# Selection and gates of a product-key expert layer by quarters of the tokens, and the sum over experts in three steps

## The chip, the cores and the metric

The kernel runs on one NeuronCore of a Trainium2 chip. Its time is the device time of one execution in microseconds (us), the median of several. Five engines execute instruction streams of their own and wait for each other through semaphores: TensorE (PE; its weight loads are listed apart, as PEld), VectorE (DVE), ScalarE (ACT), GpSimd (POOL) and SyncE (SP), which here issues the DMA transfers. Each engine works off its stream in order.

## The reference

Two layers. Each adds a token mixer (window attention, stick-breaking attention and gated linear attention beside each other) to the activations of 16 meta and 1024 real tokens, 1024 wide, and then a PEER layer with 4096 experts. Only the PEER layer matters here:

```python
q = (xt @ wq).reshape(t, 8, 2, 128)
s = jnp.einsum('thpd,hpnd->thpn', q, sub_keys)             # 8 heads, 2 halves, 64 keys
s_top, i_top = lax.top_k(s, 16)
cand_s = s_top[:, :, 0, :, None] + s_top[:, :, 1, None, :] # 16 x 16 candidates of a head
best_s, best_j = lax.top_k(cand_s, 16)
g = jax.nn.softmax(best_s, axis=-1)                        # 8 x 16 gates of a token
h_all = xt @ u.T                                           # 4096 hidden values of a token
a = gelu(h_sel) * g                                        # those of the 128 selected experts
w = zeros((t, 4096)).at[token, idx].add(a)
out = w @ v                                                # the sum over experts
```

All products are in float32. The kernel computes all 4096 hidden values of every token, multiplies them with a gate that is zero for an expert that is not selected, and sums over all experts.

## The kernel before

A float32 product is computed as three products of operands split in a high and a low part. `wpiece` loads a 128 x 512 piece of weights; ACT rounds it to the high part (L272) and POOL or DVE subtracts to get the low part (L279; `split_on` says which engine). A piece with a key is kept: its low part goes to memory and is loaded again at the next use, and ACT rounds again (L306).

The 1040 tokens stand in four quarters (272, 256, 256, 256; in the last layer the first is 256, since the meta tokens are dropped). After the attention of a layer its PEER layer goes over a first pair of quarters, P, and then a second, Q. For each pair there are these stages:

- `apply` writes the norm of a quarter (DVE L373 and L377, ACT L376).
- `scores` multiplies it with the keys (PE L977) in four blocks of two heads each, c = 0 to 3, and ACT copies the result to SBUF (L982).
- `route` selects, for one block and both quarters: the sixteen largest of each list of 64 (DVE L994 to L998, five instructions to a list), the candidates (L1010 to L1017), their sixteen largest, the softmax (Exp on ACT, L1029) and the numbers of the experts (L1047 to L1082).
- `hidden`: 32 rounds of 128 experts. PE L1101 multiplies both quarters at once, 24 matmuls of 512 columns to a round; ACT takes the Gelu (L1107, L1110), and where a token's gate is there already, POOL multiplies it in (L1108).
- `slots` transposes the selected numbers and gates (PE L1120 to L1125, DVE L1122 to L1129).
- `gates` makes the gates of 16 tokens for all experts: DVE compares the numbers with a ramp (L1140, 128x2048; L1143, 128x512; L1145, 128x1024), PE forms the outer products in 32 matmuls of 32 columns (L1152), and DVE multiplies them into the hidden rows that are there (L1157), ACT copies them for those that are not (L1159). A pair of 512 tokens has 32 such blocks.
- `values` sums over the experts for four output tiles, d0 to d0 + 3, at a time, with 32 rounds: ACT and DVE split the 128x512 gated rows (L1185, L1186), PE L1191 multiplies with 12 matmuls, and at the end DVE adds the result to the activations (L259) and POOL sums squares for the next norm (L255).

For P, all of `route` and `slots` come ahead of round 17 of hidden (PR), and the 32 gate blocks are spread over rounds 17 to 28 (PEND is 29, and what is due by then is issued at the end of a round). The norms, scores and `route` of Q are laid between the rounds of the two values passes of P, one work item to EVERY / 4 = 6 rounds: norms at rounds 6 and 12, the scores at 18, 24, 30 and 36 of 64. `route` goes between them in portions (BUD). For Q, `slots` comes after round HQ = 6 of hidden and the gates are spread to round 31 (QE). A scheduler that works at build time orders the instructions of each engine from these programs by its own estimates of their times; on the chip the order is fixed. PSUM banks are handed out by rings, named in `set_rings`: h for hidden, g for gates and slots, s and d for scores, v for values.

Of the kernel before, what the change touches and what calls it, by code (L numbers as in the profile page):

```python
# [61 lines left out]
def tile_trunk(ctx, tc, h0, w_pk, wgate, w2, glab, w_out, wqT, keysT, u_pk, v_w, sinks,  # L62
# [52 lines left out]
    kb, bb = place["keep"][1], place["beta"][1]  # L115
    place["hq"] = [1, [kb[0]], 0]
# [54 lines left out]
    set_rings(d=(0, 1), o=(2,), a=(3, 4, 5, 6, 7), h=(0, 1, 6, 7), g=(2, 3), s=(2, 3, 4, 5), v=(4, 5, 6, 7, 2, 3))  # L171
# [762 lines left out]
    def peer_setup(qa, qb):  # L934

        P = Layer()
        P.sp = sp = Span(qa.c0, qb.c1)
# [18 lines left out]
    def scores(l, P, c, halves, ring):  # L956

        sp = P.sp
        if P.s[c] is None:
            P.s[c] = sb([128, P.ns, len(sp.tiles), 4, 64], F32, "s")[:, c % P.ns]  # L960
            if sp.meta:
                POOL.memset(P.s[c][:, 0], 0.0)
# [454 lines left out]
```

## Time and profile before

| | |
|---|---|
| median of 3 runs | 3347.84 us (3345.78 to 3351.06) |
| profiled execution | 3347.21 us, span 3345.5 us |
| PE busy | 3140.4 us, 94% |
| DVE busy | 2107.7 us, 63% |
| ACT busy | 1311.3 us, 39% |
| POOL busy | 938.1 us, 28% |
| granted TensorE clock, mean | 0.961 of 2.4 GHz |

Times in the trace are from the start of the span. Layer 0 has P's hidden stage at 765 to 1045, P's values at 1045 to 1306, Q's hidden at 1306 to 1523 and its values, with the first projection of layer 1, to 1785. Layer 1 has the same stages at 2426, 2684, 2930 and 3143 us, to the end. A row of a group of instructions gives its line, engine, operation, output and input by the program's names, shapes, count, busy time and mean ns, and then the idle time of the engine ahead of it with what ended that. A share of busy time is an average over stages with different limits, so the rows below are by stage.

### The profile page before, as it was taken

Reading aid. Unit: us, or ns where it says so; the run is one execution under the profiler, and the core shown is the slowest. Engines: PE = TensorE matmul, PEld = TensorE weight load, DVE = VectorE, ACT = ScalarE, POOL = GpSimd, SP = SyncE. Lnnn points to the kernel's source line nnn. Section 1 sums busy time; section 2 is a strip of 40 time slices with the busy share of each in tenths; the row PEclk is TensorE's granted clock in tenths of the full one; section 3 lists DMA queues with packets and bytes.
Section 4 is the critical chain, followed back from the end, with each engine's and each line's share of the span. In section 5 each row is a group of like instructions: output and inputs, shape, how many; then the busy total and the mean of one; then the engine's idle time right before and its main releaser. Section 6 shows DMA issues by size and latency. Waiting matters only on the chain.

```text
span 3345.5 us, 65752 instructions
## 1 busy us (share of the span) xinstructions
PE 3140.4 (94%) x23483; PEld 2642.3 (79%) x23483; DVE 2107.7 (63%) x6764; ACT 1311.3 (39%) x3021; POOL 938.1 (28%) x963
## 2 busy tenths in 40 slices
PE   7999999989799989999998999999898899999998
PEld 7686887679799988888875868876776778688788
DVE  4645436569997589653325464465697867975447
ACT  4544324433223434324344343245342244333345
POOL 4314021214344233010311131223143433311125
PEclk9899999989899999999997999999898999999999
DMA  8767774655335655446874677756754366554655
GB/s 290 228 208 245 238 261 135 199 188 187 124 117 158 183 178 190 155 152 200 311 251 151 216 263 238 253 160 201 233 177 139 115 181 219 182 187 145 194 177 160
DMA packets 397225, 651.36 MB, mean 195 GB/s; under 512 B 43536, under 2 KB 109152, under 8 KB 396896
## 3 DMA queue, kind: packets, MB, share of 16 engines
q1 hardware_dynamic: 396896, 647.16, 60.1%
q8 instruction: 184, 3.01, 0.4%
q14 instruction: 145, 1.19, 0.1%
HBM read 489.56 MB, written 157.42 MB: 193 GB/s over the span
## 4 chain that ended last, share of the span: by engine, by line
PE 61%; DVE 21%; DMA 6%; ACT 2%; issue 2%; POOL 1%; SPq 0%; DVEq 0%; POOLq 0%; ACTq 0%
PE b L1191 15%; PE b L1101 14%; PE b L333 11%; PE b L977 4%; PE b L1152 3%; PE b L703 2%; DVE arena_r L1186 2%; DMA arena<-h 2%; DVE arena L995 2%; DVE arena L996 2%; PE b L757 1%; DVE arena L998 1%; PE b L618 1%; DVE arena L1140 1%; DVE arena L1145 1%
## 5 line engine op out<-in xcount | busy, mean ns | idle before, releaser
L279 POOL TENSOR_TENSOR arena_r<-arena,arena_r 128x512 fp32r<-128x512 f32 (+1 forms) x453 | 557.6, 1238 | 915.0 <-ACT arena_r L272 843.8
L1101 PE MATMUL b<-arena_r 128*128 128x512 f32 (+2 forms) x3840 | 766.4, 359 | 22.9 <-ACT arena L1110 13.4
L1191 PE MATMUL b<-arena_r 128*128 128x512 f32 (+2 forms) x4224 | 752.5, 337 | 31.9 <-DVE arena_r L1186 22.1
L1191 PEld LDWEIGHTS b<-arena_r 128*128 128x128 f32 x4224 | 642.6, 190 | 128.9 <-DVE arena_r L1186 37.2
L1101 PEld LDWEIGHTS b<-arena_r 128*128 128x128 f32 x3840 | 630.7, 193 | 123.0 <-ACT arena L1110 14.0
L333 PE MATMUL b<-arena_r 128*128 128x256 f32 (+1 forms) x4992 | 700.9, 294 | 27.5 <-ACT arena_r L272 6.3
L333 PEld LDWEIGHTS b<-arena_r 128*128 128x128 f32 x4992 | 641.0, 195 | 67.1 <-issue 20.4
L272 ACT ACTIVATE arena_r<-arena 128x512 fp32r<-128x512 f32 x456 | 285.0, 629 | 447.3 <-PE b L1101 93.7
L1186 DVE TENSOR_TENSOR arena_r<-arena,arena_r 128x512 fp32r<-128x512 f32 (+2 forms) x352 | 258.1, 743 | 215.6 <-ACT arena_r L1185 214.8
L306 ACT ACTIVATE arena_r<-arena 128x512 fp32r<-128x512 f32 x284 | 178.5, 631 | 359.8 <-PE b L1191 118.0
L977 PE MATMUL b<-arena_r 128*128 128x256 f32 (+1 forms) x1632 | 219.1, 290 | 17.9 <-DMA arena_r<-m_0l 6.4
L977 PEld LDWEIGHTS b<-arena_r 128*128 128x128 f32 (+1 forms) x1632 | 204.2, 190 | 30.9 <-DMA arena_r<-m_0l 8.5
L1140 DVE TENSOR_TENSOR arena<-arena 128x2048 f16<-128x2048 f16 x129 | 172.4, 1338 | 59.7 <-PE b L1152 59.7
L1108 POOL TENSOR_TENSOR arena<-arena 128x272 f32<-128x272 f32 (+26 forms) x86 | 90.0, 1051 | 372.5 <-ACT arena L1159 177.5
L1185 ACT ACTIVATE arena_r<-arena 128x512 fp32r<-128x512 f32 (+2 forms) x352 | 171.8, 502 | 24.1 <-PE b L1191 24.1
L1152 PEld LDWEIGHTS <-arena 128*128 128x128 f16 x4128 | 144.9, 118 | 36.9 <-DVE arena L1145 20.8
L1152 PE MATMUL b<-arena 128*128 128x32 f16 x4128 | 154.0, 190 | 18.9 <-DVE arena L1145 18.8
L255 POOL TENSOR_TENSOR arena<-arena 128x256 f32<-128x256 f32 (+2 forms) x105 | 90.7, 864 | 260.5 <-ACT arena L254 256.0
L715 DVE TENSOR_TENSOR_SCAN arena<-arena,zf 128x384 f32<-128x384 f32 (+6 forms) x116 | 104.5, 904 | 82.0 <-ACT arena L710 81.0
L279 DVE TENSOR_TENSOR arena_r<-arena,arena_r 128x256 fp32r<-128x256 f32 (+1 forms) x187 | 98.0, 528 | 89.7 <-ACT arena_r L272 72.0
L421 ACT ACTIVATE arena<-b 128x256 f32<-128x256 f32 (+1 forms) x144 | 55.4, 385 | 212.3 <-PE b L333 211.8
L1157 DVE SCALAR_TENSOR_TENSOR arena<-b,arena 128x288 f32<-128x288 f32 (+21 forms) x129 | 63.7, 499 | 111.6 <-PE b L1152 111.6
(268 smaller groups left out, 3877.9 us busy)
## 6 DMA issues: line engine op xcount, KB each, us to landing
arena<-in_v_w_dram SPq DMA_DIRECT2D x288, 256.0 KB, 2.9
arena<-in_u_pk_dram SPq DMA_DIRECT2D x256, 256.0 KB, 3.0
arena_r<-a_0h SPq DMA_DIRECT2D x108, 256.0 KB, 3.6
arena_r<-a_0l SPq DMA_DIRECT2D x108, 256.0 KB, 3.9
arena_r<-a_1h SPq DMA_DIRECT2D x108, 256.0 KB, 3.0
arena_r<-a_1l SPq DMA_DIRECT2D x108, 256.0 KB, 3.5
arena<-m SPq DMA_DIRECT2D x92, 256.0 KB, 4.4
arena<-in_w_pk_dram SPq DMA_DIRECT2D x72, 256.0 KB, 4.3
```

The costliest lines, as they stand in the source:

```text
L272: ACT.activation(hi, src, AF.Copy)
L279: e.tensor_tensor(lo[:, a:b], src[:, a:b], hi[:, a:b].bitcast(F32), op=ALU.subtract)
L306: ACT.activation(hi, wload(src), AF.Copy)
L333: PE.matmul(ps, wt[:, ks], x.at(low, k, xo, sp.w), start=(k == 0 and i == 0), stop=(k == KT - 1 and i == 2))
L715: DVE.tensor_tensor_scan(keep[0:m, 0:wd][:, ::-1], keep[0:m, 0:wd][:, ::-1], zf[0:m, 0:1].to_broadcast([m, wd]), keep[0:m, wd:wd + 1], op0 ...
L977: PE.matmul(ps, yv(half, low, k, oo, m), wt[:, kk * 256:kk * 256 + 256], start=(k == 0 and i == 0 and e == 0), stop=(k == KT - 1 and i == ...
L1101: PE.matmul(ps, wt[:, ks], yv(h, low, k, 0, w // 2 if h is None else w), start=(k == 0 and i == 0), stop=(k == KT - 1 and i == 2))
L1140: DVE.tensor_tensor(Lh, iotaM.unsqueeze(1).to_broadcast([128, 4, 128, 4]), v4(P.mT, 128), op=ALU.is_equal)
L1152: PE.matmul(ps[:, i * 32:(i + 1) * 32], Lh[:, b, :, t], R[:, b, part, :, t], start=(part == 0), stop=(part == 1))
L1185: ACT.activation(ah, G[:, r, o:o + w], AF.Copy)
L1186: last = DVE.tensor_tensor(al, G[:, r, o:o + w], ah.bitcast(F32), op=ALU.subtract)
L1191: PE.matmul(ps, wt[:, d * 128:d * 128 + 128], pr[low], start=(opens and r == 0 and i == 0), stop=(closes and r == 31 and i == 2))
```

## The change

Selection goes by quarter and by two pairs of heads (`tops`, `combine`) instead of by pair of quarters and by score block. The gate blocks of a pair's first quarter stay in `hidden`, from round 15 to 30; those of its second quarter (`second`) go into the first pass of values, which then handles the first quarter only. The sum over experts has three steps: output tiles 0 to 3 for the first quarter, tiles 4 to 7 for both quarters, and tiles 0 to 3 for the second. The weights of tiles 0 to 3 are loaded and split afresh in each of these steps (`reuse=False`). Value matmuls of 512 columns go from 1920 to 1152, those of 256 from 1536 to 3072. The norms of both quarters of Q are at round 1 of the first values pass and its score blocks at rounds 8, 14, 20 and 26 of it; its selection is in the second and third pass and inside Q's hidden stage. The bank rings are new. The low parts of the weights are on POOL throughout the PEER layer, but for Q's second and third step, where POOL and DVE share a piece. The attention is not touched.

```diff
-BUD = 0.3
 LAG = 1
-EVERY = 24
-HQ = 6
-PR = 17
+PR = 15
 START = 0
 MM = ((3, 0, 2, 0, 0, 3, 0, 0), (3, 0, 2, 0, 0, 3, 0, 0))
-PEND = 29
-QE = 31
+PEND = 31
...
-    set_rings(d=(0, 1), o=(2,), a=(3, 4, 5, 6, 7), h=(0, 1, 6, 7), g=(2, 3), s=(2, 3, 4, 5), v=(4, 5, 6, 7, 2, 3))
+    set_rings(d=(0, 1), o=(2,), a=(3, 4, 5, 6, 7), h=(6, 7, 2, 3), g=(0, 1), s=(4, 5), v=(4, 5, 6, 7, 2, 3))
...
+    def tops(P, half, cc):
+
+        nt = len(P.parts[half][1].tiles)
+        V = sb([128, 3, 8, 16], F32, "V")
+        I = sb([128, 3, 8, 16], U32, "I")
+        P.V[half, cc] = V, I
+        for a in range(8):
+            for j in range(nt):
+                top16(sv(P, half, 2 * cc + a // 4)[:, j, a % 4, :], V[:, j, a], I[:, j, a])
+                yield 1.3
...
+    def combine(P, half, cc, startT, pidxT):
+
+        nt = len(P.parts[half][1].tiles)
+        ng = 4 * nt
+        z = "s" if half else ""
+        V, I = P.V.pop((half, cc))
...
+            w0 = P.parts[0][1].w
+            while cst and P.gated[0] < w0 and P.gated[0] * (end - lo) < w0 * (r + 1 - lo):
+                gates(P, 0, G, *cst)
...
+    def second(P, G, cst):
+
+        while P.gated[1] < P.parts[1][1].w:
+            gates(P, 1, G, *cst)
+            yield 3.0
+
+    def values(l, P, G, halves, d0, todo=iter(()), work=(), bud=0.0, hs=None, reuse=True):
...
+            if r in work:
+                work.pop(r)()
+            if len(done) > LAG:
+                left += bud
+                with tc.issue_after(done[-1 - LAG]):
+                    while left > 0:
+                        left -= next(todo, 99)
...
-        scores(l, P, P.ns - 1, (0,), "s")
+        scores(l, P, 3, (0,), "s")
...
+        def run(*gens):
+            for _ in itertools.chain(*gens):
+                pass
+
+        for c in range(3):
             scores(l, P, c, (1,), "s")
-            with tc.issue_after(A.done):
-                route(P, c, startT, pidxT)
-        hidden(l, P, G, 0, 4, "h")
-        for c in range(P.ns, 4):
-            scores(l, P, c, (0, 1), "s")
-            route(P, c, startT, pidxT)
-        hidden(l, P, G, 4, PR, "h")
-        slots(P)
+        with tc.issue_after(A.done):
+            run(tops(P, 0, 0), combine(P, 0, 0, *tabs), tops(P, 0, 1))
+            scores(l, P, 3, (1,), "s")
+            run(combine(P, 0, 1, *tabs))
+        hidden(l, P, G, 0, PR, "h")
+        slots(P, 0)
+        run(tops(P, 1, 0), tops(P, 1, 1))
         hidden(l, P, G, PR, 32, "h", cst, PEND)
+        run(combine(P, 1, 0, *tabs), combine(P, 1, 1, *tabs))
+        slots(P, 1)
         Q = peer_setup(qs[2], qs[3])
-        split_on(POOL)
-        todo = iter(())
-        work = [lambda: apply(2 * l + 1, qs[2], gf, Y[0], rb), lambda: apply(2 * l + 1, qs[3], gf, Y[1], rb2)]
-        work += [lambda c=c: scores(l, Q, c, (0, 1), "d") for c in range(4)]
-        step = 0
-        done = []
-        for d in (0, 4):
-            for last in values_steps(l, P, G, (0, 1), d):
-                done.append(last)
-                step += 4
-                if work and step >= EVERY:
-                    work.pop(0)()
-                    step = 0
-                    if len(work) < 4:
-                        todo = itertools.chain(todo, route_steps(Q, 3 - len(work), startT, pidxT))
-                if len(work) < 4:
-                    left = BUD * 4
-                    with tc.issue_after(done[-1 - LAG]):
-                        while left > 0:
-                            left -= next(todo, 9)
-        for _ in todo:
-            pass
-        split_on(POOL)
-        hidden(l, Q, G, 0, HQ, "h")
-        slots(Q)
-        split_on(*QSPL)
-        hidden(l, Q, G, HQ, 32, "h", cst, QE)
+        scored = []
+
+        def norms():
+            apply(2 * l + 1, qs[2], gf, Y[0], rb)
+            apply(2 * l + 1, qs[3], gf, Y[1], rb2)
+
+        work = {6 * c + 8: lambda c=c: scored.append(scores(l, Q, c, (0, 1), "g")) for c in range(4)}
+        work[1] = norms
+        todo = values(l, P, G, (0,), 0, second(P, G, cst), work, 2.2, reuse=False)
+        run(todo)
+        todo = itertools.chain(tops(Q, 0, 0), combine(Q, 0, 0, *tabs), tops(Q, 0, 1), combine(Q, 0, 1, *tabs))
+        todo = values(l, P, G, (0, 1), 4, todo, (), 1.8)
+        todo = values(l, P, G, (1,), 0, todo, (), 0.8, reuse=False)
+        run(todo)
+        hidden(l, Q, G, 0, PR, "h")
+        slots(Q, 0)
+        run(tops(Q, 1, 0), tops(Q, 1, 1))
+        hidden(l, Q, G, PR, 32, "h", cst, PEND)
+        run(combine(Q, 1, 0, *tabs), combine(Q, 1, 1, *tabs))
+        slots(Q, 1)
         more = l + 1 < DEPTH
         if more:
             rb = rstd(2 * l + 2, quarters[0])
             apply(2 * l + 2, quarters[0], g_attn[:, l + 1], XR[0], rb)
-        split_on(POOL, POOL, DVE, POOL)
+        todo = second(Q, G, cst)
+        run(itertools.islice(todo, 5))
+        todo = values(l, Q, G, (0,), 0, todo, (), 2.0, reuse=False)
+        run(todo)
         if more:
-            values(l, Q, G, (0, 1), 0)
             L = attn_layer(l + 1)
             pr = proj_span(l + 1, L, quarters[0], XR[0])
             A = next(pr)
             split_on((POOL, DVE))
             rb = rstd(2 * l + 2, quarters[1])
...
+            values(l, Q, G, (0, 1), 4)
             next(pr)
-            values(l, Q, G, (0, 1), 4)
+            values(l, Q, G, (1,), 0, reuse=False)
...
+        split_on((POOL, DVE))
+        values(l, Q, G, (0, 1), 4, work={2 + 8 * i: lambda i=i: final(qs[i]) for i in range(2)}, hs=hs)
...
+        values(l, Q, G, (1,), 0, work={4: lambda: final(qs[2])}, hs=hs, reuse=False)
```

The first place where the order moves is DVE in layer 1 while PE computes the first scores of P; L373 and L377 are the norm of P's second quarter, L355 and L360 the preparation of its factors. Before:

```order
L355 TENSOR_SCALAR arena<-b_66 128x2 x2
L360 TENSOR_SCALAR arena<-ident,arena 128x128 x3
L373 SCALAR_TENSOR_TENSOR arena<-arena,g_ffn 128x256
L360 TENSOR_SCALAR arena<-ident,arena 128x128
L377 TENSOR_TENSOR arena_r<-arena,arena_r 128x256
L373 SCALAR_TENSOR_TENSOR arena<-arena,g_ffn 128x256
L377 TENSOR_TENSOR arena_r<-arena,arena_r 128x256
L373 SCALAR_TENSOR_TENSOR arena<-arena,g_ffn 128x256 x2
```

In the change the same norm is L379 and L383, and L997 to L1001, L1041 to L1087 and L1064 are selection:

```order
L999 MATCH_REPLACE arena<-arena 128x64 x2
L1064 SCALAR_TENSOR_TENSOR arena<-arena 128x16x8
L1046 RECIPROCAL arena<-arena 128x8
L379 SCALAR_TENSOR_TENSOR arena<-arena,g_ffn 128x256
L1081 TENSOR_TENSOR arena<-arena 128x256x8
L1000 MAX arena<-arena 128x8 x8
L1065 TENSOR_SCALAR arena<-arena 128x16x8
L1047 TENSOR_TENSOR arena<-arena 128x2x64
L379 SCALAR_TENSOR_TENSOR arena<-arena,g_ffn 128x256 x2
L383 TENSOR_TENSOR arena_r<-arena,arena_r 128x256
```

The norm stood as a closed group between the selection before it and after it; it now has selection instructions among its own.

The second place is DVE in layer 1 where P's hidden ends and its values begin. L1140, L1145 and L1157 are the end of the last gate blocks, L1186 low parts, L373 and L377 the norm of Q's first quarter. Before:

```order
L1140 TENSOR_TENSOR arena<-arena 128x2048
L1145 TENSOR_TENSOR arena<-arena 128x1024
L1157 SCALAR_TENSOR_TENSOR arena<-b_68,arena 128x29x16
L1157 SCALAR_TENSOR_TENSOR arena<-b_67,arena 128x29x16
L1186 TENSOR_TENSOR arena_r<-arena,arena_r 128x512 x2
L373 SCALAR_TENSOR_TENSOR arena<-arena,g_ffn 128x256
L377 TENSOR_TENSOR arena_r<-arena,arena_r 128x256
L373 SCALAR_TENSOR_TENSOR arena<-arena,g_ffn 128x256
```

In the change L1172 is the product of a gate block, L1206 a low part (256 wide), L379 and L383 the norm, L1136 to L1143 the slots and L1155, L1158 and L1160 the gate blocks of the second quarter:

```order
L1172 SCALAR_TENSOR_TENSOR arena<-b_65,arena 128x31x16
L383 TENSOR_TENSOR arena_r<-arena,arena_r 128x256
L1206 TENSOR_TENSOR arena_r<-arena,arena_r 128x256 x4
L379 SCALAR_TENSOR_TENSOR arena<-arena,g_ffn 128x256 x2
L383 TENSOR_TENSOR arena_r<-arena,arena_r 128x256 x2
L1136 COPY arena<-b_66 128x128
L1137 COPY arena<-b_66 128x128
L1155 TENSOR_TENSOR arena<-arena 128x2048 x2
L1158 TENSOR_TENSOR arena<-arena 128x512 x2
L1143 SCALAR_TENSOR_TENSOR arena<-b_65,arena 128x32x4
```

No gate block was left here; now the slots and gate blocks of the second quarter stand among the norms and the low parts.

The third place is ACT at the start of P's hidden in layer 1. L1110 is a Gelu, L1029 an Exp of `route`, L272 the high part of a weight piece. Before, the second of four Exps:

```order
L272 ACTIVATE arena_r<-arena 128x512 x2
L1110 ACTIVATE arena<-b_65 128x512
L272 ACTIVATE arena_r<-arena 128x512 x2
L1110 ACTIVATE arena<-b_66 128x512
L272 ACTIVATE arena_r<-arena 128x512
L1029 ACT_TABLE_LOAD
L1029 ACTIVATE arena<-arena 128x128
L272 ACTIVATE arena_r<-arena 128x512
L1110 ACT_TABLE_LOAD
```

In the change L1124 is the Gelu, L1043 the Exp, L278 and L312 high parts of weights and L993 the copy of scores:

```order
L1043 ACTIVATE arena<-arena 128x128
L312 ACTIVATE arena_r<-arena 128x512 x4
L993 ACTIVATE arena<-b_70 128x512
L278 ACTIVATE arena_r<-arena 128x512 x4
L993 ACTIVATE arena<-b_69 128x512
L278 ACTIVATE arena_r<-arena 128x512 x3
L1124 ACT_TABLE_LOAD
L1124 ACTIVATE arena<-b_71 128x512
```

The first two of the four Exps now stand ahead of the first Gelu, where before one stood after the first, sixth, tenth and thirteenth Gelu.

## Rows read from the trace of the kernel before

**Rows 1.** Page, part 1: busy us, share of the span, instructions.

```profile
PE 3140.4 (94%) x23483; PEld 2642.3 (79%) x23483; DVE 2107.7 (63%) x6764; ACT 1311.3 (39%) x3021; POOL 938.1 (28%) x963
```

**Rows 2.** Busy time by stage: from:to, length, engines in turn, clock, DMA.

```profile
765.00:1045.30 280.30, 253.50 (x2730) 249.55 (x2729) 258.35 (x900) 85.43 (x202) 126.16 (x89) 0.95 0.41 133
1045.30:1306.50 261.20, 244.77 (x1928) 238.86 (x1927) 197.10 (x931) 106.00 (x249) 88.58 (x68) 0.98 0.59 181
...
2426.40:2683.70 257.30, 224.13 (x1806) 182.61 (x1804) 223.70 (x741) 80.17 (x161) 113.33 (x78) 0.91 0.43 139
2683.70:2930.20 246.50, 236.10 (x1167) 193.77 (x1168) 191.32 (x884) 97.44 (x183) 92.22 (x65) 0.98 0.64 200
2930.20:3143.40 213.20, 213.20 (x1794) 174.65 (x1793) 127.13 (x287) 74.72 (x166) 26.80 (x28) 1.00 0.52 164
...
2377.50:2409.50 32.00, 25.83 (x181) 24.20 (x180) 11.17 (x33) 13.55 (x30) 6.24 (x8) 0.84 0.89 292
```

**Rows 3.** PE's waits, 2426 to 2684: us in total, times, longest.

```profile
PE b L1152 <- DVE arena L1145: 13.3, 8, 3.0
PE b L1120 <- DVE arena L1080: 9.1, 1, 9.1
PE b L1101 <- ACT arena_r L272: 7.7, 2, 5.5
```

**Rows 4.** PE's waits, 765 to 1045.

```profile
PE b L1101 <- ACT arena L1110: 13.4, 3, 5.6
PE b L1120 <- DVE arena L1080: 7.8, 1, 7.8
```

**Rows 5.** PE's instructions in time: start us, us, line, operation, [idle before].

```profile
1530.28 73.94 PE L1191 MATMUL b<-arena_r 128*128 128x512 f32 x320
...
2661.91 1.25 PE L1152 MATMUL b<-arena 128*128 128x32 f16 x32 [3.02 <-DVE arena L1145]
...
2680.91 1.25 PE L1152 MATMUL b<-arena 128*128 128x32 f16 x32 [1.02 <-DVE arena L1145]
...
2741.78 9.29 PE L977 MATMUL b<-arena_r 128*128 128x256 f32 x77
...
3053.10 5.83 PE L1101 MATMUL b<-arena_r 128*128 128x512 f32 x24
3058.77 1.25 PE L1152 MATMUL b<-arena 128*128 128x32 f16 x32
...
3242.51 42.08 PE L1191 MATMUL b<-arena_r 128*128 128x256 f32 x356
```

**Rows 6.** ACT's instructions in time: the fourth Exp of layer 1's P.

```profile
2524.96 0.31 ACT L1029 ACTIVATE arena<-arena 128x128 f32<-128x128 f32 x1 [14.83 <-DVE arena L1028]
```

**Rows 7.** DVE's instructions in time: end of the norm of P's second quarter.

```profile
2405.01 0.43 DVE L377 TENSOR_TENSOR arena_r<-arena,arena_r 128x256 fp32r<-128x256 f32 x1 [0.48 <-ACT arena_r L376]
```

**Rows 8.** Busy time by engine, 2560 to 2683.

```profile
2560.00:2683.00 123.00, 108.86 (x1336) 91.71 (x1334) 99.08 (x124) 32.76 (x83) 56.36 (x38) 0.92 0.36 118
```

**Rows 9.** DVE's groups of instructions, 2560 to 2683.

```profile
L1145 DVE TENSOR_TENSOR arena<-arena 128x1024 f16<-128x1024 f16 x30 | 29.6, 988 | 0.0
L1143 DVE TENSOR_TENSOR arena<-arena 128x512 f16<-128x512 f16 x28 | 21.1, 783 | 0.0
```

**Rows 10.** Single DVE lines, whole span: ns min/median/max.

```profile
L1145 DVE TENSOR_TENSOR arena<-arena x129: 675/683/1794, 912.8 to 3126.8; 128x1024 f16<-128x1024 f16 x129
...
L1143 DVE TENSOR_TENSOR arena<-arena x129: 405/412/1534, 911.2 to 3121.6; 128x512 f16<-128x512 f16 x129
...
L1186 DVE TENSOR_TENSOR arena_r<-arena,arena_r x352: 395/691/1782, 986.7 to 3329.2; 128x512 fp32r<-128x512 f32 x80, 128x272 fp32r<-128x272 f32 x59, 128x256 fp32r<-128x256 f32 x37
...
L373 DVE SCALAR_TENSOR_TENSOR arena<-arena,g_ffn x64: 457/482/1603, 559.4 to 2714.0; 128x256 f32<-128x256 f32 x56, 128x272 f32<-128x272 f32 x8
...
L377 DVE TENSOR_TENSOR arena_r<-arena,arena_r x128: 396/418/1891, 19.9 to 2715.3; 128x256 fp32r<-128x256 f32 x104, 128x272 fp32r<-128x272 f32 x24
```

**Rows 11.** POOL's groups of instructions, 2684 to 2930.

```profile
L279 POOL TENSOR_TENSOR arena_r<-arena,arena_r 128x512 fp32r<-128x512 f32 x59 | 83.5, 1418 | 131.8 <-ACT arena_r L272 111.7 <-DMA arena<-in_v_w_dram 18.2 <-DMA arena<-h 1.8
```

**Rows 12.** POOL's groups of instructions, whole span, shapes apart.

```profile
L255 POOL TENSOR_TENSOR arena<-arena 128x256 f32<-128x256 f32 x77 | 59.8, 777 | 167.1 <-ACT arena L254 165.1 <-DMA arena<-in_h_dram 1.4 <-DMA o_1h<-arena_r 0.6
```

**Rows 13.** PE's waits, 3143 to the end.

```profile
PE b L1191 <- DVE arena_r L1186: 3.4, 4, 1.2
```

More of the change, by code (lines that the diff above doesn't have):

```diff
@@ L956, in scores @@
     def scores(l, P, c, halves, ring):
[L958 to L962, printed above, removed]
-        own = [(j, o, m) for j, (o, m) in enumerate(sp.tiles) if (1 if o >= P.parts[1][0] else 0) in halves]
-        own.sort(key=lambda t: -t[2])
-        pairs = [own[i:i + 2] for i in range(0, len(own), 2)]
+        pairs = []
+        for half in halves:
+            tiles = list(enumerate(P.parts[half][1].tiles))
+            if len(tiles) == 3:
+                POOL.memset(sv(P, half, c)[:, 0], 0.0)
+                pairs.append((half, tiles[0:1]))
+            pairs.append((half, tiles[-2:]))
         bks = [ps1(ring) for _ in pairs]
@@ L968, in scores @@
             wh, wl = wpiece(m_scr[l][c][:, kq * 512:(kq + 1) * 512], f"m{l}_{c}_{kq}")
-            for bk, pair in zip(bks, pairs):
-                for e, (j, o, m) in enumerate(pair):
-                    half = 1 if o >= P.parts[1][0] else 0
-                    oo = o - P.parts[half][0]
+            for bk, (half, tiles) in zip(bks, pairs):
+                for e, (j, (o, m)) in enumerate(tiles):
                     ps = bk[0:m, e * 256:e * 256 + 256]
@@ L976, in scores @@
                         for i, (low, wt) in enumerate(((0, wh), (0, wl), (1, wh))):
-                            PE.matmul(ps, yv(half, low, k, oo, m), wt[:, kk * 256:kk * 256 + 256],
+                            PE.matmul(ps, yv(half, low, k, o, m), wt[:, kk * 256:kk * 256 + 256],
                                       start=(k == 0 and i == 0 and e == 0),
-                                      stop=(k == KT - 1 and i == 2 and e == len(pair) - 1))
-        for bk, pair in zip(bks, pairs):
-            for e, (j, o, m) in enumerate(pair):
-                ACT.activation(P.s[c][0:m, j], bk[0:m, e * 256:e * 256 + 256].rearrange("p (a n) -> p a n", a=4), AF.Copy)
@@ new lines, in scores, with top16 @@
+        for bk, (half, tiles) in zip(bks, pairs):
+            j, m, n = tiles[0][0], tiles[0][1][1], len(tiles)
+            ACT.activation(sv(P, half, c)[0:m, j:j + n], bk[0:m, 0:n * 256].rearrange("p (j a n) -> p j a n", a=4, n=64),
+                           AF.Copy)
+    def top16(s, val, idx):
+        DVE.max(val[:, 0:8], s)
+        DVE.max_index(idx[:, 0:8], val[:, 0:8], s)
+        DVE.match_replace(s, val[:, 0:8], s, -3.0e38)
+        DVE.max(val[:, 8:16], s)
+        DVE.max_index(idx[:, 8:16], val[:, 8:16], s)
@@ L1111, in hidden, with slots @@
             P.rows = r + 1
-            while cst and P.gated < P.sp.w and P.gated * (end - lo) < P.sp.w * (r + 1 - lo):
-                gates(P, G, *cst)
-    def slots(P):
-        sp = P.sp
-        for j, (o, m) in enumerate(sp.tiles):
+            w0 = P.parts[0][1].w
+            while cst and P.gated[0] < w0 and P.gated[0] * (end - lo) < w0 * (r + 1 - lo):
+                gates(P, 0, G, *cst)
+    def slots(P, half):
+        for j, (o, m) in enumerate(P.parts[half][1].tiles):
             tp = ps1("g").bitcast(F16)[:, 0:256].rearrange("p (a b) -> p a b", a=2)
@@ L1270, in tile_trunk @@
             if q == 3:
-                for c in range(P.ns - 1):
+                for c in range(3):
                     scores(l, P, c, (0,), "d")
```

199 lines of the change are left out of this document (97 added, 102 removed).

## The prediction

> **What bounds the kernel now.** I read the busy shares first, then busy time by stage, then PE's waits in the stages whose length exceeds its work, and last the single instructions that end those waits. TensorE (PE) is busy 94% of the span [rows 1], so almost only its idle or slowed time can be won. By stage [rows 2] that time is not spread evenly. The hidden stage of the second pair in layer 1 (2930 to 3143) is all PE at full clock: 213.20 of 213.20 us. The same stage of the first pair (2426 to 2684) does no more PE work and takes 257.30: 224.13 busy, granted clock 0.91. So 44.1 us are lost there, and about 12.5 of them are no wait but PE running slower. The waits [rows 3] are: the slot transposes for the end of selection on VectorE (DVE), 9.1; fresh weights behind ScalarE (ACT), 7.7; the gate matmuls for DVE, 13.3. ACT is itself held: its queue holds each softmax Exp ahead of weight copies, and an Exp for which DVE has not finished idles ACT 14.83 us [rows 6]. Layer 0 shows the same, 13.4 for the Gelu and 7.8 for the slots [rows 4]. In that stage DVE is the late engine, since selection of 512 tokens and 32 gate blocks fall into it. In the two values stages of first pairs [rows 2] PE is busy 236.10 of 246.50 and 244.77 of 261.20.
>
> **Unit prices.** A hidden round of 24 matmuls starts 5.67 us before the gate block that follows it (3053.10 to 3058.77) [rows 5], so 32 rounds are 181.6. The rest of the 213.2 is 31.6 for 32 gate blocks: 0.99 each on PE. Values matmuls: 73.94/320 = 0.231 for 512 columns, 42.08/356 = 0.118 for 256. A score block of 96 is 96 x 9.29/77 = 11.6 [rows 5]. Where PE waits for every gate block, seven come in 2680.91 - 2661.91 = 19.0 us [rows 5]: 2.71 each on DVE.
>
> **Hidden of the first pair.** Sixteen gate blocks leave it, and the selection behind which it waited is halved in front of the slots. Layer 1: 181.6 + 15.8 = 197.4. ACT's order now has two Exps before the first Gelu and the third behind five; I take their waits as gone, because DVE works on selection in 22 us that it now idles. But the second quarter's norm, which before stood as a closed group, now stands among selection instructions. In the profile DVE is busy only 11.17 of the 32.0 us around it [rows 2], and the last product of that norm is at 2405.01 [rows 7]. Filling the 21 us of gaps pushes it, and with it scores and hidden, back by up to 20.8; I take 20 (bounds 0 and 35: none or all of the selection that the order puts between its first and last row, each instruction at its duration in the profile, falls ahead of it). So 217.4 for 257.3: **-40**. Layer 0: 528 columns, 181.6 x 528/512 = 187.3, 17 blocks 16.8, the 120 score matmuls that stay in the stretch 14.5, late start 6 (its norm has fewer selection rows around it): 224.6 for 280.3: **-56**.
>
> **Hidden of the second pair.** Sixteen gate blocks fewer, PE is the bound, 15.8 in each layer: **-32**. Selection of its second half lies beside 197 us of PE; if that cover failed, the slots would wait as in [rows 3], 9.
>
> **Values of the first pair.** Pass 1 now holds on PE 384 x 0.118 = 45.4, 16 gate blocks 15.8 and four score blocks 46.4: 108. In the new order the first score block stands behind 120 values matmuls and five gate blocks and is itself mixed with gates; about 31 us of PE work end with it. On DVE its end needs 8 gate blocks, 14 low parts and 32 norm instructions, because the norms are issued at round 1. That is 8 x 2.71 = 21.7, 14 x 0.395 = 5.5 and 16 x (0.482 + 0.418) = 14.4 [rows 5, 10]: 41.6.
>
> The price of a GpSimd (POOL) subtraction beside DVE has to be added. From 2560 to 2683 POOL ran 38 instructions [rows 8]. In that stretch L1145 took 988 on the mean where its median over the kernel is 683, and L1143 783 where it is 412 [rows 9, 10]: 30 x 0.305 + 28 x 0.371 = 19.5 us over 38, so 0.51 per POOL instruction. The bounds are 0 (POOL falls into gaps) and the 1.42 of a whole POOL instruction [rows 11]. With 14 of them the first part is 41.6 + 7.1 = 48.7, and PE waits 48.7 - 31 = 18. The later 77 us of PE cover what DVE has left (8 blocks, 18 low parts, 38 us with POOL). Pass 1 is 108 + 18 + 3 at its start = 129. Pass 2 is 384 x 0.231 + 3 = 91.7. Pass 3 has 45.4 on PE, but POOL has 32 fresh low parts at 1.42 and eight squares at 0.777 [rows 11, 12], 51.7, and 3 us of start: 55. The sum is 275.7 for 246.5: **+29**. In layer 0 passes 1 and 2 are 272 wide on one half (+2.7 each): 281.1 for 261.2: **+20**.
>
> The Trainium skill, page "SBUF — State Buffer", has as its single rule that VectorE and GpSimd take a shared port pair as an exclusive lock, the loser blocked until the other's instruction ends. The lengthened L1143 and L1145 agree in kind; the trace's 0.51 is well under a whole instruction. By that rule in full, this change goes to the third rival below.
>
> **Values of the second pair.** Pass 1 was 512 wide with nothing else; now 45.4 of values and 15.8 of gates on PE stand against 16 x 2.71 + 32 x 0.395 + 32 x 0.51 = 72.3 on DVE, and the slots and the start, 4.5. The gates run through the whole pass on PE's queue, so PE waits in order: 77 where the sum alone took 45.4. Other passes have the same columns. **+32** in layer 0, and +28 in layer 1, where 3.4 of wait on L1186 go [rows 13].
>
> **The clock.** PE lost 12.5 us to the lower level per 31.6 of waits in the stage above. The new waits, 18 + 18 + 20 + 6 = 62 in the first pairs, would cost 25 at that share; I take 10, because PE is not idle for long in any of them (bounds 0 and 25).
>
> **Sum.** -40 - 56 - 32 + 29 + 20 + 32 + 28 + 10 = -9. The profiled execution is 3347.2 us, 0.6 under the median 3347.84, so the median should be **3339**.
>
> **Rivals.**
> First, a lighter POOL: its pieces fall into DVE's gaps. The 92 pieces that were charged (14 and 32 in each layer) give back 92 x 0.51 = 47: 3292. For it: most DVE instructions of the profile run at their median, and the order mixes low parts and gates. Against it: DVE has no gaps in pass 1.
> Second, the old waits stay. If the third and fourth Exp still hold ACT, 9.1 + 7.7 + 13.4 + 7.8 = 38 [rows 3, 4] stay and the late start of 26 falls away: 3351, no change. For it: ACT keeps an Exp among weight copies. Against: DVE begins selection of these quarters earlier.
> Third, slower: in pass 1 of both pairs VectorE becomes the bound, because each POOL piece holds it for most of its length. The place is the 92 pieces; every 0.1 us more per piece is 9.2 us, so from 0.61 a piece the change loses. At 1.0 it is 92 x 0.49 = 45: 3384; at 1.42 it is 84: 3423. For it: those passes put DVE and POOL against each other with no long PE work over them. Against: the measured mean.
> That the change does not do what it says is excluded by the order: the sixteen gate blocks stand in pass 1.
>
> **How the numbers follow.** Forecast 0.40 (own range 3320 to 3356), lighter POOL 0.27, slower 0.22, old waits 0.08, others 0.03. About 0.2% (6.7 us) is what a measurement can tell. Faster: 0.24 of the forecast's, 0.27, 0.04 of the rest: 0.55. Same: 0.12 and 0.03: 0.15. Slower: 0.04, 0.21 and 0.05: 0.30. The range runs from the lighter POOL to the slower case at 1.0: 3290 to 3384.
>
> **What would show it.** Hidden of the first pairs near 217 and 225 us with no long wait on the slots; of the second pairs near 197 and all PE. In pass 1 of the first pairs one wait of about 18 us ahead of or inside the first score block; in pass 1 of the second pairs gate matmuls waiting for DVE L1160, the pass about 77. Wrong if hidden keeps its ACT waits, or if the low parts and gate instructions on DVE run at 0.4 and 2.7 in pass 1.

## The result and the profile after

The change is slower: 3391.8 us (median of 4, 3384.91 to 3396.7) beside 3349.45 for the kernel before on the same chip, a ratio of 1.0121 with a 95% interval of 1.0092 to 1.0149. The forecast was 3339 with a range to 3384. The third rival (VectorE held up by POOL's pieces in pass 1) had said 3384 at 1.0 us a piece.

From the times at which PE's lines begin and end in the two traces (spans of 3345.5 and 3394.9 us), against the forecast's terms:

| stretch | before, us | after, us | difference | forecast |
|---|---|---|---|---|
| up to the first score block | 629.4 | 632.4 | +3 | 0 |
| layer 0, first scores to the end of P's hidden | 416.1 | 376.5 | -40 | -56 |
| layer 0, P's values and Q's hidden | 477.3 | 489.9 | +13 | +4 |
| layer 0, Q's values and the attention of layer 1 | 764.5 | 809.3 | +45 | +32 |
| layer 1, first scores to the end of P's hidden | 396.4 | 350.5 | -46 | -40 |
| layer 1, P's values and Q's hidden | 459.7 | 485.7 | +26 | +13 |
| layer 1, Q's values and the end | 202.1 | 250.6 | +49 | +28 |

Another +10 of the forecast was for the clock, in no stretch. So the traces differ by +49 us where the forecast's sum was -9; the rest of this text asks where those 58 us lie. The busy time of single stages after, in the columns of [rows 2] (from:to, length, then PE, PEld, DVE, ACT and POOL with their counts, clock, DMA share, GB/s):

```profile
790.30:1008.90 218.60, 211.43 (x2092) 209.95 (x2091) 173.62 (x643) 75.80 (x179) 112.62 (x81) 0.98 0.49 159
...
2460.70:2658.60 197.90, 197.90 (x1291) 160.31 (x1290) 151.40 (x485) 69.00 (x143) 109.91 (x81) 1.00 0.54 175
2658.60:2783.30 124.70, 115.47 (x1288) 113.88 (x1286) 77.56 (x127) 49.62 (x103) 47.77 (x33) 0.93 0.49 152
2783.30:2881.10 97.80, 91.29 (x386) 72.52 (x385) 94.17 (x455) 39.93 (x71) 48.76 (x36) 0.98 0.58 185
2881.10:2943.10 62.00, 51.27 (x385) 48.60 (x384) 60.33 (x349) 31.00 (x70) 43.52 (x35) 0.94 0.57 172
2943.10:3144.30 201.20, 199.53 (x1290) 161.57 (x1290) 90.90 (x278) 68.84 (x144) 18.00 (x23) 0.99 0.56 177
3144.30:3230.90 86.60, 74.09 (x911) 72.38 (x909) 81.37 (x102) 31.35 (x69) 50.26 (x31) 0.86 0.40 115
```

These are P's hidden of layer 0, and of layer 1 P's hidden, its three values passes, Q's hidden, and Q's first pass. P's hidden, which took 257.30 with the waits of [rows 3], is now 197.90 of PE at full clock: that gain is there. The last row is the largest loss among these stages: Q's pass 1 has some 61 us of PE work and takes 86.60, in which DVE is busy 81.37 and the clock falls to 0.86. Passes 2 and 3 of P show DVE busy 94.17 of 97.80 and 60.33 of 62.00. PE's waits in Q's pass 1 (us, times, longest) end with DVE, on the last gate operation:

```profile
PE b L1167 <- DVE arena L1160: 9.7, 8, 1.9
PE b L1212 <- DVE arena_r L1206: 1.9, 1, 1.9
```

DVE's groups of that pass (xcount | busy us, mean ns | idle before) tell why DVE was late:

```profile
L1155 DVE TENSOR_TENSOR arena<-arena 128x2048 f16<-128x2048 f16 x16 | 25.5, 1597 | 0.0
L1160 DVE TENSOR_TENSOR arena<-arena 128x1024 f16<-128x1024 f16 x16 | 19.1, 1196 | 0.0
L1206 DVE TENSOR_TENSOR arena_r<-arena,arena_r 128x256 fp32r<-128x256 f32 x28 | 18.3, 676 | 0.2 <-ACT arena_r L1205 0.2
L1158 DVE TENSOR_TENSOR arena<-arena 128x512 f16<-128x512 f16 x16 | 11.4, 724 | 0.0
L1172 DVE SCALAR_TENSOR_TENSOR arena<-b,arena 128x512 f32<-128x512 f32 x16 | 10.9, 680 | 0.7 <-PE b L1167 0.7
```

The medians of L1160 and L1158 are 683 and 412 ns in [rows 10], where they are L1145 and L1143, and the shortest L1206 is 395 (there L1186). Here they take 1196, 724 and 676. L1172, which reads PSUM and one tile of SBUF, takes 680 here and 685 where POOL is nearly idle (experiment 1). In P's pass 1 of the same trace, where DVE is busy 77.56 of 124.70 us and POOL makes 32 low parts as well, the same groups are much less lengthened:

```profile
L1155 DVE TENSOR_TENSOR arena<-arena 128x2048 f16<-128x2048 f16 x16 | 22.9, 1433 | 0.0
L1206 DVE TENSOR_TENSOR arena_r<-arena,arena_r 128x256 fp32r<-128x256 f32 x28 | 12.4, 452 | 38.5 <-ACT arena_r L1205 38.5
L1160 DVE TENSOR_TENSOR arena<-arena 128x1024 f16<-128x1024 f16 x16 | 11.9, 748 | 0.0
...
L1158 DVE TENSOR_TENSOR arena<-arena 128x512 f16<-128x512 f16 x16 | 8.7, 548 | 0.0
```

### The profile page after: what moved, and what is told of

Same layout as the page of the kernel before. It is cut to its first block, busy times and chain, and to the rows that moved or that the text cites. A ratio compares the mean times of both kernels' runs of the same rounds, so it can differ in the third digit from the quotient of the medians.

```text
span 3394.9 us, 67695 instructions
## 1 busy us (share of the span) xinstructions
PE 3163.7 (93%) x24221; PEld 2704.3 (80%) x24221; DVE 2155.4 (63%) x6849; ACT 1352.9 (40%) x3095; POOL 1112.1 (33%) x1093
## 4 chain that ended last, share of the span: by engine, by line
PE 60%; DVE 21%; DMA 6%; issue 2%; ACT 2%; POOL 1%; SPq 1%; POOLq 0%; DVEq 0%; ACTq 0%
PE b L1115 19%; PE b L339 11%; PE b L1212 10%; PE b L988 4%; PE b L1167 3%; DVE arena_r L1206 3%; PE b L709 2%; DVE arena L1155 2%; DVE arena L998 2%; DMA arena<-h 2%; PE b L763 2%; DVE arena L999 1%; DVE arena L1160 1%; DVE arena L1001 1%; PE b L624 1%
## 5 line engine op out<-in xcount | busy, mean ns | idle before, releaser
L285 POOL TENSOR_TENSOR arena_r<-arena,arena_r 128x512 fp32r<-128x512 f32 (+1 forms) x584 | 753.6, 1301 | 924.9 <-ACT arena_r L278 859.2
L1212 PE MATMUL b<-arena_r 128*128 128x256 f32 (+2 forms) x4992 | 784.2, 317 | 53.5 <-DVE arena_r L1206 50.6
L1115 PE MATMUL b<-arena_r 128*128 128x512 f32 (+2 forms) x3840 | 746.2, 354 | 8.9 <-ACT arena L1124 6.2
L278 ACT ACTIVATE arena_r<-arena 128x512 fp32r<-128x512 f32 x584 | 364.8, 629 | 545.8 <-PE b L1115 111.7
L1206 DVE TENSOR_TENSOR arena_r<-arena,arena_r 128x256 fp32r<-128x256 f32 (+2 forms) x416 | 273.5, 667 | 182.5 <-ACT arena_r L1205 181.7
L312 ACT ACTIVATE arena_r<-arena 128x512 fp32r<-128x512 f32 x256 | 161.0, 631 | 379.4 <-PE b L1115 112.3
L1155 DVE TENSOR_TENSOR arena<-arena 128x2048 f16<-128x2048 f16 x129 | 184.6, 1435 | 111.5 <-PE b L1167 111.4
L1205 ACT ACTIVATE arena_r<-arena 128x256 fp32r<-128x256 f32 (+2 forms) x416 | 185.7, 455 | 63.6 <-PE b L1212 50.8
L261 POOL TENSOR_TENSOR arena<-arena 128x256 f32<-128x256 f32 (+1 forms) x126 | 103.6, 822 | 237.6 <-ACT arena L260 233.6
L285 DVE TENSOR_TENSOR arena_r<-arena,arena_r 128x256 fp32r<-128x256 f32 x188 | 104.6, 562 | 91.0 <-ACT arena_r L278 79.5
L1122 POOL TENSOR_TENSOR arena<-arena 128x16 f32<-128x16 f32 (+15 forms) x64 | 56.1, 877 | 308.8 <-ACT arena L1174 167.8
L582 POOL TENSOR_TENSOR arena<-arena,mhalf 128x8 f32<-128x8 f32 (+3 forms) x43 | 62.0, 1441 | 193.3 <-DVE arena L579 125.8
```

Of the source, the lines that this page charges most:

```text
L278: ACT.activation(hi, src, AF.Copy)
L285: e.tensor_tensor(lo[:, a:b], src[:, a:b], hi[:, a:b].bitcast(F32), op=ALU.subtract)
L312: ACT.activation(hi, wload(src), AF.Copy)
L1115: PE.matmul(ps, wt[:, ks], yv(h, low, k, 0, w // 2 if h is None else w), start=(k == 0 and i == 0), stop=(k == KT - 1 and i == 2))
L1155: DVE.tensor_tensor(Lh, iotaM.unsqueeze(1).to_broadcast([128, 4, 128, 4]), v4(P.mT[half], 128), op=ALU.is_equal)
L1205: ACT.activation(ah, G[:, r, o:o + w], AF.Copy)
```

## The experiments

Theory A: in Q's pass 1 a POOL subtraction keeps DVE's instructions with two SBUF inputs waiting, and DVE becomes the bound. Theory B: the pass is long because of its order, gate block behind gate block. Theory C, for P's passes 2 and 3: DVE's selection bounds them. Ratios are to the kernel before, measured again beside each group of runs; its median was 3349 to 3354 us, so two experiments are compared by their ratios.

**1. Q's pass 1 without POOL** (keys instead of `reuse=False`, in P's pass 1, which stores the low parts, and in Q's, which loads them):

```diff
-values(l, P, G, (0,), 0, second(P, G, cst), work, 2.2, reuse=False)
+values(l, P, G, (0,), 0, second(P, G, cst), work, 2.2)
-values(l, Q, G, (0,), 0, todo, (), 2.0, reuse=False)
+values(l, Q, G, (0,), 0, todo, (), 2.0)
```

> The first values pass of the second pair takes the low parts of its weights kept from the first pair's first pass, so POOL has no subtraction there (and the first pair's pass 1 stores 32 pieces more). Theory A: POOL subtractions hold up DVE in that pass (0.88 us for each of 31 in layer 1, 0.70 in layer 0). Then DVE's sum there falls from 88.9 to 62 to 66 us, the pass from 86.6 to 66 to 70 in layer 1 and by some 20 in layer 0: about 3352 us, 40 less than the change. Theory B: the pass is long because 16 gate blocks stand behind each other on DVE and PE waits for them in order, POOL or not (62 us uncontended plus the waits between PE and DVE). Then the pass stays at 80 to 87: 3380 to 3395.

Measured: 3350.73, ratio 0.9987 (0.997 to 1.0004), no difference from the kernel before and some 45 us below the change. The pass takes 65.40 instead of 86.60 in layer 1 and 91.70 instead of 115.20 in layer 0. The same DVE groups in layer 1:

```profile
L1155 DVE TENSOR_TENSOR arena<-arena 128x2048 f16<-128x2048 f16 x16 | 19.9, 1249 | 0.0
L1206 DVE TENSOR_TENSOR arena_r<-arena,arena_r 128x256 fp32r<-128x256 f32 x28 | 11.3, 418 | 4.3 <-ACT arena_r L1205 4.3
...
L1160 DVE TENSOR_TENSOR arena<-arena 128x1024 f16<-128x1024 f16 x16 | 10.8, 683 | 0.0
L1158 DVE TENSOR_TENSOR arena<-arena 128x512 f16<-128x512 f16 x16 | 6.5, 416 | 0.0
```

and the pass itself:

```profile
3123.30:3188.70 65.40, 64.89 (x910) 64.29 (x909) 55.95 (x102) 31.14 (x69) 2.72 (x3) 1.00 0.80 262
```

The sixteen gate blocks and their order are the same. With POOL at 2.72 us instead of 50.26, DVE's four groups are 25.8 us shorter (74.3 to 48.5), PE is the bound again and the clock is 1.00. Theory B falls. Of the 31 POOL instructions of the pass (28 low parts, three others), the 28 low parts are gone and the other three are still there, so the price is 25.8/28 = 0.92 for each low part.

**2. The low parts of that pass on DVE instead of POOL** (`split_on(DVE)` ahead of it, `split_on(POOL)` behind):

> The second pair's pass 1 has its low parts on DVE in place of POOL; all else is the change. Theory A says that POOL's help is worth nothing there, since each piece holds DVE up for nearly as long as DVE would need for it: DVE has 61.6 us of its own and 32 x 0.69 = 22 more, 84 for the 88.9 measured with POOL, and the time stays within 8 us of the change: 3384 to 3396. Rival: POOL works beside DVE and the lengthening has another cause (waits for data, the order); then 22 us more on DVE make each layer's pass longer by 15 to 22: 3420 to 3435.

Measured: 3365.28, ratio 1.0035 (1.0022 to 1.0048): some 29 us faster than the change, better than theory A's forecast of the change's time within 8 us. In the traces 21 of them lie in the two passes: 86.60 to 77.70 in layer 1 and 115.20 to 103.20 in layer 0. The groups of the pass:

```profile
L285 DVE TENSOR_TENSOR arena_r<-arena,arena_r 128x512 fp32r<-128x512 f32 x28 | 18.7, 676 | 0.0
L1206 DVE TENSOR_TENSOR arena_r<-arena,arena_r 128x256 fp32r<-128x256 f32 x28 | 11.2, 410 | 0.0
...
L1160 DVE TENSOR_TENSOR arena<-arena 128x1024 f16<-128x1024 f16 x16 | 10.7, 676 | 0.0
```

A low part costs DVE 0.676 us to make and 0.92 us to have made by POOL (experiment 1). With experiment 1 that settles A: POOL's help was worth less than nothing there. DVE is busy 73.14 of the 77.70 us.

**3. Q's second gates back in hidden.** Q's `slots` come at rounds 6 and 20, and the gate blocks of its first quarter are spread over rounds 6 to 19, of its second over 20 to 31 (`hidden` takes the quarter as an argument). In this run alone, Q's selection of the second quarter works on scores that have been overwritten; instructions and shapes are those of the full work.

> The second pair's gate blocks of its second quarter go back into its hidden stage (first quarter's at rounds 6 to 19, second's at 20 to 31); the three steps stay. Theory A: DVE works alone there, since POOL has 18 us in 201; hidden grows by the 15.8 us of PE for 16 blocks, pass 1 falls from 86.6 to 48 to 52: 20 less in each layer, about 3350. Theory B says the same of pass 1, so this run tells only whether hidden has room; if DVE is late there (selection of the second quarter and 32 blocks are about 170 us against 213), the stage grows by 30 and more: 3375 or above.

Measured: 3376.63, ratio 1.0064 (1.0042 to 1.0086), some 19 us below the change by the ratios, with hidden at 216.6 and pass 1 at 47.8 in layer 1:

```profile
3150.30:3198.10 47.80, 46.81 (x399) 46.51 (x396) 41.21 (x35) 27.79 (x60) 40.91 (x30) 1.00 0.62 177
```

The pass went as expected, though POOL has 40.91 us in it: beside low parts alone DVE has room. Of the 23 us that hidden and pass 1 give together in layer 1, 8 were lost again in the later passes.

**4. Less selection in P's passes 2 and 3** (half of that of Q's first quarter is called after pass 3; budgets 1.2 and 0.4 instead of 1.8 and 0.8):

> Half of the selection of the second pair's first quarter moves from passes 2 and 3 of the first pair into the second pair's hidden stage, where DVE is busy 91 of 201 us. Theory C: passes 2 and 3 are bound by DVE (94 of 97.8 and 60 of 62.0 us busy in layer 1). Then pass 2 goes to about 92 and pass 3 to 50 to 54, 14 to 18 us less in each layer, and hidden stays at 201: about 3362. Rival: they are bound by POOL's fresh low parts (48 in 97.8, 44 in 62.0) or by the 256-wide matmuls; then nothing changes, 3385 to 3395.

Measured: 3390.81, ratio 1.0101 (1.0077 to 1.0124), no gain. It is no test of pass 3: the scheduler issued the rest of the selection early. In layer 1 pass 2 fell from 97.80 to 93.80, but DVE was busy 67.80 of 67.80 us in pass 3:

```profile
2873.50:2941.30 67.80, 52.02 (x387) 48.17 (x385) 67.80 (x323) 33.02 (x74) 45.25 (x35) 0.97 0.56 167
```

**5. The same half held** until the last low part of pass 3:

```diff
+with tc.issue_after(P.last):          # P.last: the last low part of the last pass
+    run(tops(Q, 0, 1), combine(Q, 0, 1, *tabs))
```

> The second half of the selection of the second pair's first quarter may not be issued before the last low part of the first pair's pass 3 (in the run before this, the scheduler pulled it forward again, and DVE stayed busy 67.8 of 67.8 us in pass 3). Theory C: passes 2 and 3 of the first pair are bound by DVE. Then pass 2 goes from 97.8 to 91 to 94 and pass 3 from 62 to 48 to 52, hidden of the second pair stays at 201: 14 to 20 us less a layer, 3352 to 3364. Rival: POOL's 32 fresh pieces (44 us busy in 62) and what they hold up set pass 3; then it stays above 56 and the time above 3375.

Measured: 3380.83, ratio 1.0083 (1.0056 to 1.011). In layer 1 pass 2 fell to 93.4, as C says. Pass 3 hardly did: 59.4, with DVE busy 55.73 in far fewer instructions, and the low parts L1206 at 946 ns where they took 649 in the change:

```profile
2874.60:2934.00 59.40, 49.41 (x385) 47.30 (x383) 55.73 (x111) 31.12 (x70) 47.26 (x35) 0.97 0.58 181
```

```profile
L1206 DVE TENSOR_TENSOR arena_r<-arena,arena_r 128x256 fp32r<-128x256 f32 x31 | 28.4, 946 | 3.5 <-ACT arena_r L1205 3.5
```

349 DVE instructions took 60.33 us, and 111 take 55.73: without the selection DVE is nearly as long busy, since POOL's 32 pieces now lengthen the low parts more. So C is wrong for pass 3 as the only cause.

**6. All third steps with kept low parts** (no `reuse=False` at all):

> All third steps take kept low parts too, so POOL subtracts only in the first pair's passes 1 and 2. Theory A: without POOL beside it DVE needs 64 us less the 7.5 us of lengthening in pass 3 of the first pair, 54 to 56 instead of 62, and the second pair's pass 3 loses its 28 DVE halves (17 us) but PE sets it, 47 to 50 for 53.5: 3335 to 3342, 10 to 16 less than with pass 1 alone. Rival: a round of pass 3 then loads 512 KB in 1.42 us, 370 GB/s, as much as the most that any stretch shows (365 at a DMA share of 1.03); then pass 3 grows to 60 and more and the time is 3350 to 3365.

Measured: 3345.92, ratio 0.9986 (0.9967 to 1.0004), the same as with Q's pass 1 alone. P's pass 3 with selection but with POOL at 4.87 and 5.37 us, in layers 0 and 1:

```profile
1241.10:1298.10 57.00, 48.45 (x387) 46.05 (x385) 53.63 (x387) 31.11 (x69) 4.87 (x7) 1.00 0.93 316
...
2856.80:2916.70 59.90, 49.65 (x386) 46.33 (x384) 57.02 (x396) 32.45 (x72) 5.37 (x7) 0.98 0.92 310
```

It was 62.00 in both layers of the change. PE's waits in it now end with ACT's high parts of the kept weights (L312) more than with DVE's low parts, here in layer 0:

```profile
PE b L1212 <- ACT arena_r L312: 4.8, 5, 1.5
PE b L1115 <- ACT arena_r L312: 1.8, 1, 1.8
PE b L1212 <- DVE arena_r L1206: 1.5, 3, 0.8
```

**7. Q's pass 1 with kept low parts and the held half** (1 and 5):

> Both: kept low parts in the second pair's pass 1 and the held selection. If theories A and C are both right the gains add: 41 and some 30, 3318 to 3325, faster than the kernel before by 0.8% or so. If one covers the other: 3340 to 3352.

Measured: 3349.24, ratio 0.999 (0.9972 to 1.0009): the gains do not add. Beside experiment 1, pass 2 of P is 101.50 us for 103.70 in layer 0 and 93.30 for 97.90 in layer 1, pass 3 is 61.60 for 61.00 and 61.50 for 64.40, and P's pass 1 of layer 1 took 3.2 back (127.30 for 124.10).

**8. All kept and the held half** (5 and 6):

> All third steps take kept low parts, and half of the selection of the second pair's first quarter is held until after the first pair's pass 3. In pass 3 of the first pair two loads lay on DVE, selection and POOL's pieces beside it; with one taken away each run before still showed DVE busy 56 to 57 of 59 us. If that is the whole story, pass 3 with both away is set by PE: 47 to 51 us, and the time 3328 to 3338, some 12 below the kernel with kept low parts alone. Rival: the loads of 512 KB a round (share 0.92 in pass 3 with kept low parts) take over, or the held selection delays the second pair's slots: 3342 to 3352.

Measured: 3331.99, ratio 0.9933 (0.9914 to 0.9952), faster than the kernel before. Pass 3 of layers 0 and 1:

```profile
1237.10:1288.70 51.60, 49.17 (x385) 47.44 (x386) 31.25 (x112) 29.87 (x64) 7.86 (x7) 0.97 0.95 326
...
2839.70:2897.90 58.20, 49.35 (x385) 46.13 (x383) 35.90 (x147) 31.77 (x70) 6.74 (x7) 0.99 0.93 313
```

DVE is idle for over a third of both. In layer 0 PE sets the pass: 59.60 with POOL's pieces alone (experiment 5), 57.00 with selection alone (6) and 51.60 with neither, so there each load had been enough to keep the pass late. In layer 1 the three are 59.40, 59.90 and 58.20: taking both away gave next to nothing. PE's waits there show both parts of the expectation's rival, the loads and the held selection, which now holds up the start of Q's hidden:

```profile
PE b L1115 <- DVE arena L1000: 3.2, 1, 3.2
PE b L1213 <- DMA arena_r<-v_0l: 3.0, 5, 1.0
PE b L1213 <- ACT arena_r L312: 1.5, 2, 1.0
```

The time is the one expected, but not for the reason given: beside experiment 6, pass 3 gives 5.4 and 1.7 us, and pass 2, now with half the selection, 5.0 (102.40 to 97.40) and 8.1 (99.40 to 91.30).

**9. Selection by quarters alone**: all gate blocks in hidden (P: first quarter from round 15, second from 24; Q as in 3, but from round 8 and on intact scores), two steps of both quarters, norms and scores of Q at rounds 6 to 36 as before.

> Selection by quarters alone: all 32 gate blocks of a pair are in hidden again (second quarter's from round 24 in the first pair, from 20 in the second), the sum over experts has two steps of both quarters. If the loss is in the moved gates and the third step, this has the change's shorter hidden stage without its price: hidden of the first pair 198 + 16 + the late start = 225 to 232 for 257 and 280, the values as before: 3285 to 3310. Rival: the second quarter's 16 blocks then come late on DVE (43 us behind its selection in 8 rounds of 6.7 us), PE waits for them at the end of hidden as it did before, and the time is 3330 to 3350.

Measured: 3339.11, ratio 0.9967 (0.9947 to 0.9986), slightly faster than the kernel before; the rival's time. After the last round of P's hidden in layer 1, PE still waits for gates:

```profile
2433.20:2651.10 217.90, 212.50 (x1614) 173.71 (x1612) 180.69 (x524) 71.02 (x148) 111.22 (x79) 0.98 0.50 162
2651.10:2672.10 21.00, 7.48 (x192) 6.87 (x192) 20.77 (x29) 3.88 (x13) 7.64 (x4) 0.63 0.23 67
```

So this version, with selection by quarters and the gates in hidden, gains 11 us, and the change is some 52 slower than it by the ratios. The moved gates, the third step with its fresh weights and the earlier norms and scores of Q lie in those 52 together; no run takes them apart but for the 45 us of experiment 1, which took the fresh low parts out of Q's pass 1.

**10. P as in 6, Q as in 9:**

> First pair as in the change, but with kept low parts in its pass 3; second pair with all gate blocks in hidden and two steps of both quarters, as in the kernel before. The first pair's hidden is shorter by some 40 in each layer than in the kernel before and its values longer by 25 to 30, the second pair as before: 3315 to 3330, below both kernels. Rival: with the first pair's pass 3 still bound by DVE's selection, the first pair gains nothing on balance: 3340 to 3350.

Measured: 3336.52, ratio 0.9945 (0.9929 to 0.996), between the expectation and its rival. In layer 1 P's hidden and values take 485.0 us together, for 503.8 in the kernel before.

**11. As 8, with P's second gates issued more slowly in pass 1** (1.5 instead of 2.2):

> The version with all low parts kept and the held selection, and with the second quarter's gate blocks of the first pair issued more slowly in pass 1 (0.5 instead of 0.73 of a block to a round), so that in layer 1 six instead of eight stand ahead of the end of the first score block. If pass 1 (123.6 us for 108 of PE work) waits there because DVE has gate blocks to do ahead of the norms' last products, two blocks fewer take 5 to 6 us from it in each layer: 3320 to 3328. Rival: the norms themselves come late (loads of the stored rows), or the gates are then late at the end of the pass: 3330 to 3340.

Measured: 3321.05, ratio 0.9904 (0.9883 to 0.9926), the lowest ratio, 1.0% below the kernel before; its interval overlaps that of experiment 8. The mechanism is not shown: pass 1 of P is 125.00 us in layer 1 (123.60 in 8) and 127.60 in layer 0 (131.00), and the rest of the difference is spread over stretches that the edit does not touch.

## Why the prediction was wrong

- **The failing step** is the price of a POOL subtraction beside DVE, 0.51 us, carried from a stretch of P's hidden [rows 8, 9], in which DVE was busy 99.08 of 123 us, to Q's pass 1. There DVE was busy 81.37 of 86.60 us and the price was 0.92: experiment 1 shows it, and experiment 2 agrees. "77 where the sum alone took 45.4" was 86.6. That is the third rival's mechanism, and its point of no return, 0.61 a piece, was passed in Q's pass 1. Of the 58 us this is 10 in layer 1 and at most the 13 of its stretch in layer 0.
- **The price was also read too low.** Of the 38 POOL instructions by which the lengthening was divided, 27 were subtractions and 11 the products of Gelu and gate (L1108), down to 128x48; and L1140 in the same stretch, 1261 ns for a median of 1214, was left out:

```profile
L1140 DVE TENSOR_TENSOR arena<-arena 128x2048 f16<-128x2048 f16 x30 | 37.8, 1261 | 0.0
...
L279 POOL TENSOR_TENSOR arena_r<-arena,arena_r 128x512 fp32r<-128x512 f32 x27 | 41.0, 1519 | 37.8 <-ACT arena_r L272 36.3 <-DMA u_0l<-arena_r 1.3
```

  That makes 20.9 us: 0.55 over all 38, and 0.77 if the subtractions bear it alone. That the price grows with DVE's busy share is a reading of three stretches, not a test: 0.2 a piece in P's pass 1 (DVE 62% busy; 7.0 us over 33 POOL instructions, the four groups shown above against their means in experiment 1), 0.55 to 0.77 here (81%) and 0.92 in Q's pass 1 (94%).
- **P's pass 1** came out as added up, 124.70 for 129, partly by luck. Its part up to the end of the first score block took the forecast 48.7 us and the rest 76.00 for 77, but not by one wait of 18 us: PE waited 8.9 in five pieces and was slower for the rest, at a mean clock of 0.82, and 10 POOL instructions lay there, not 14:

```profile
2658.60:2707.30 48.70, 39.85 (x447) 38.53 (x445) 43.19 (x76) 18.37 (x44) 16.02 (x10) 0.82 0.44 131
2707.30:2783.30 76.00, 75.62 (x847) 75.34 (x845) 34.38 (x51) 31.25 (x60) 31.76 (x24) 1.00 0.53 165
```

- **Passes 2 and 3 of P** were mis-sized. Pass 2 had no term for DVE at all (91.7, PE alone), and pass 3 was charged to POOL alone (55). They took 97.80 and 62.00 in layer 1, 102.90 and 62.00 in layer 0, together some 29 us over the forecast. In pass 2 it was DVE's load, busy 94.17 of 97.80: half the selection less gave 4 to 6.5 us in layer 1 (experiments 5 and 8); POOL's pieces stayed in it in every run. In pass 3 of layer 0 each of selection and POOL's pieces kept it late (experiments 5, 6 and 8). In layer 1 that is not shown: with both gone it is 58.20.
- **Q's stages**: hidden fell by 20 us in layer 0 and 12 in layer 1, for 16 in each; Q's values cost 93 where 60 was forecast. Of these 33, 10 are pass 1 of layer 1; the rest lies in pass 3 (53.60 for 45.4), the end, and layer 0's pass 1, which shares its stretch with the first projection and was not split further.
- **P's hidden** was right in layer 1: length 197.90 for 197.4, start 13.5 late for 20. In layer 0 it began 22.0 late for 6, but 14.5 of that are the 120 score matmuls, counted inside the stretch, that now all stand ahead of hidden. Its length was 218.60 for 204 without them, of which one wait for a Gelu is 6.2; for most of the rest the hidden matmuls were busy 195.38 for 187.3, at a mean clock of 0.98, and why is open.
- **The clock**: the +10 was not seen as a term of its own. Where PE waits in Q's pass 1 the mean granted clock is 0.86 of 2.4 GHz, and 1.00 in experiment 1, where the waits are gone.
- The Trainium skill, page "SBUF — State Buffer", section "Who interferes with whom", has as its single rule an exclusive lock of the shared port pair, which VectorE's instructions with two SBUF inputs contend for. Experiment 1 agrees in kind: of the pass's five large groups only those with two SBUF inputs were lengthened (L1172, with one input from PSUM, is at 680 with POOL and 685 without), and the price of 0.92 is below the 1.705 of a whole piece.

Not settled: what makes DVE late in the first part of P's pass 1, what holds P's pass 3 in layer 1, and why Q's later passes give back 8 us of experiment 3.

## What to carry to other kernels

A price for two engines in each other's way holds for how busy they are where it was read; moved to a pass where the later one has hardly a gap, it was higher here. Read it with the right divisor, and over all the groups that it touches. Before work is moved off a late engine's stage, add up what the receiving stage already gives that engine's neighbours to do: here 16 gate blocks met 32 POOL pieces. Where two loads each keep an engine late, taking one away shows little, as in P's pass 3 of layer 0; take both before the theory is dropped.

## What the runs showed of the hardware

A 128x512 subtraction of float32 that DVE does itself cost it 0.676 us, and 0.92 us when POOL did it beside DVE's gate operations; POOL's own piece took 1418 ns in [rows 11] and 1705 there, so the instructions of both engines were lengthened:

```profile
L285 POOL TENSOR_TENSOR arena_r<-arena,arena_r 128x512 fp32r<-128x512 f32 x28 | 47.3, 1705 | 24.3 <-ACT arena_r L278 22.9 <-PE b L1212 1.1
```
